# Low parts of input weights: subtracted on GpSimd, or added by a transfer onto a negated copy

## Chip, cores and metric

One NeuronCore of a Trainium2 chip. The metric is device time in microseconds of one execution; the median of three runs is given, and one more execution is profiled.

## What is computed

A trunk of two layers on 512 tokens of 1024 features, in float32. Each layer projects its input `x` by one matrix of 4300 columns into the queries, keys and values of three groups of attention heads (differential, top-128 sparse with an index scorer, forgetting) and a gate. Queries and keys of the first two groups are rotated (rope). The gated outputs go through one output matrix and a layer norm.

```python
def hybrid_layer(x, w_in, ...):
    h = jnp.einsum('bsd,de->bse', x, w_in)
    (dq, dk, dv, sq, sk, sv, iq, ik, iw, fq, fk, fv, ff, gate) = split_columns(h)
...
    mixed = jnp.concatenate([a, bo, co], axis=-1) * jax.nn.silu(gate.astype(jnp.float32))
    out = jnp.einsum('bse,ed->bsd', mixed.astype(x.dtype), w_out)
    return layer_norm(DEEPNORM_ALPHA * x + out, ln_g, ln_b)
```

The time of each layer begins with the einsum on `w_in`, whose weights are what the change touches.

## The kernel before, in words

Every matmul on weights is done in three passes: input and weight are each split into a high part (rounded to `F32R`) and a low part (the rest), and high times high, low times high and high times low are summed in PSUM. So each weight block needs a high tile `whi` and a low tile `wlo`.

`Weights.prep` (line 499) prepares one block of `w_in`, at most 128 x 1024 numbers, 512 KB: SP loads it into `raw` (`dma`, line 364), ScalarE writes `whi` from `raw` (`act`, line 337), and `split` (line 386) has `wlo = raw - whi` computed by whichever of VectorE and GpSimd would end first by the planner's account (`either`, line 377; GpSimd is preferred by a bias, `PREP_BIAS` for most blocks). There are two `raw`, four `whi` and four `wlo` buffers. `prefetch` (line 544) prepares a block three groups ahead of its use. `columns` and `v_group` (lines 553 and 647) issue the matmuls of a group once its parts are ready; the value groups `dv` and `fv` consist of two or three blocks that are needed one right after the other. The output weights have a preparation of their own (`prep_out`, line 514), with `split`.

The work of a layer starts with the groups of `HEAD`: shared keys, `dk`, `dq`, `dv`, then the index queries `iq` 1, 0, 3, 2. `rope` (line 615) turns a projection into query or key tiles: ScalarE copies PSUM to a `tg` tile, SP exchanges its 32-row blocks by four small transfers, products and sums with cosine and sine run on VectorE and GpSimd, and `query_tiles` or `key_tiles` (lines 581 and 591) split the result into `qk` tiles, the low parts on GpSimd or VectorE. `forget` (line 808) runs some twenty tiny operations on `lt` tiles on GpSimd. `index_scores` (line 866) takes the `iq` tiles in order and is the first to need `iq` 0.

All five engines run in an order written down beforehand. `Flow` (line 107) plays the program through: tasks of different priority issue instructions, `issue` (line 221) gives each a start by when its operands and its engine are free, and at the end every engine's instructions are emitted by planned start (`emit`, line 236). On the chip each engine takes its instructions in that order, and each waits for its operands' semaphores; one that waits holds up what is behind it on its engine.

Of the kernel before, what the change touches and what calls it, by code (L numbers as in the profile page):

```python
# [10 lines left out]
AF = mybir.ActivationFunctionType  # L11
OP = mybir.AluOpType
# [37 lines left out]
PREP_BIAS = 3500  # L50
# [56 lines left out]
class Flow:  # L107
# [113 lines left out]
    def issue(self, engine, cost, outs, ins, emit, size=0, port=False):  # L221

        t = max(self.now, self.depends(engine, outs, ins))
        if engine == "pe":
            self.cold = self.cold or t + COLD
            self.now = t + (cost if t >= self.cold else 2 * cost)
        else:
            t = self.slot(engine, t, cost, port)
        end = t + cost
        if engine == "sp":  # L230
            end = self.slot("dma", end + 650, size / 360.0) + size / 360.0
        self.record(engine, end, outs, ins)
        self.order.append((t, len(self.order), emit))
        return end + {"pe": 0, "act": 300, "dve": 260, "pool": 200, "sp": 1040}[engine]

    def emit(self):
        for _, _, f in sorted(self.order, key=lambda o: o[:2]):
# [57 lines left out]
def tile_hybrid_decoder(  # L295
# [17 lines left out]
    nc = tc.nc  # L313
# [8 lines left out]
    flow = Flow()  # L322


    def width(ap):
        n = 1
        for d in ap.shape[1:]:
            n *= d
        return n

    def is_ap(v):
        return isinstance(v, bass.AP)

    def in_psum(ap):
        return ap.tensor.name.split("_")[0] in BANKS

    def act(o, i, func=AF.Copy, **kw):
        acc = [kw["accum_out"]] if "accum_out" in kw else []
        ptr = [v for k, v in kw.items() if is_ap(v) and k != "accum_out"]
        cost = 0.833 * width(o) + (51 if in_psum(i) else 93) + 93 * (len(acc) + len(ptr)) + (125 if o.shape[0] < 128 else 0)  # L340
        return flow.issue("act", cost, [o] + acc, [i] + ptr,
                          lambda: nc.scalar.activation(o, i, func, **kw))  # L342
# [9 lines left out]
    def two_ports(name, o, ins):  # L352

        if name == "scalar_tensor_tensor" and len(ins) == 3:
            ins = [ins[0], ins[2]]
        if name in ("tensor_tensor", "scalar_tensor_tensor"):
            return len(ins) == 2 and not any(in_psum(v) for v in ins)
        return name in ("tensor_scalar", "tensor_copy") and width(o) % 2 == 0 and not any(in_psum(v) for v in ins + [o])
# [5 lines left out]
    def dma(o, i):  # L364
        inside = [v for v in (o, i) if not v.tensor.name.startswith(("in_", "out_"))]
        outs, ins = [v for v in inside if v is o], [v for v in inside if v is i]
        return flow.issue("sp", 640 if ins else 475, outs, ins, lambda: nc.sync.dma_start(o, i),  # L367
                          width(o) * o.shape[0] * 4)

    def mm(o, lhsT, rhs, **kw):  # L370
        flow.issue("pe", width(o) / 2.262 + 2, [o], [lhsT, rhs],
                   lambda: nc.tensor.matmul(o, lhsT, rhs, **kw))  # L372
# [4 lines left out]
    def either(o, a, b, op, bias=BIAS):  # L377

        def end(engine, cost):
            port = engine == "pool" or two_ports("tensor_tensor", o, [a, b])  # L380
            return flow.free_at(engine, max(flow.now, flow.depends(engine, [o], [a, b])), cost, port) + cost
        late = in_psum(a) or in_psum(b) or \
            end("pool", 2.15 * width(o) + 125) > end("dve", 1.04 * width(o) + 69) + bias
        return (vec if late else pool)("tensor_tensor", o, a, b, op=op)

    def split(hi, lo, src, bias=BIAS):
        flow.set("high", act(hi, src))
        return either(lo, src, hi.bitcast(F32), OP.subtract, bias)

    def bank(tag):  # L390
        tag = SHARE.get(tag, tag)
        flow.banks[tag].remove(min(flow.banks[tag]))
        return flow.tile(ps.tile([128, 512], F32, name=tag, tag=tag, bufs=BANKS[tag]), tag, 0, True)

    def tile_of(shape, tag, bufs=0, dt=F32):
        n = bufs or RINGS[tag]
        return flow.tile(sb.tile([128] + shape, dt, name=tag, tag=tag, bufs=n), tag, n, not bufs)
# [45 lines left out]
    def xT_from(l, t, src, ready):  # L443
        for kk in range(2):
            yield "at", ready[kk]
            yield "bank", "t", 1
            pt = bank("t")
            for k in range(4):
                transpose(pt[:, k * 128:(k + 1) * 128], src[kk][:, k * 128:(k + 1) * 128])
            p3 = pt.rearrange("p (k n) -> p k n", k=4)  # L450
            r = split(xh[:, kk * 4:kk * 4 + 4, t * 128:(t + 1) * 128],
                      xl[:, kk * 4:kk * 4 + 4, t * 128:(t + 1) * 128], p3)
            flow.unbank("t", pt)
            yield
        flow.set(("xT", l, t), r)

    def warm():

        z0, z = small([256], "junk", 2)[:, :128], tile_of([256], "junk", 2, F32R)[:, :128]
        vec("memset", z0, 0.0, rate=0.52)  # L460
        yield "at", vec("tensor_copy", z, z0)
        yield "bank", "t", 1
        o = bank("t")[:, :256]
        while "started" not in flow.ev:
            mm(o, z, z[:, :1].to_broadcast([128, 256]), start=True, stop=True)
            yield
        flow.unbank("t", o)

    def load_x():
        yield "take", "pt", NB  # L470
        tiles, at = [], {}
        for k in range(KT):
            if k % 2 == 0:
                tiles.append(tile_of([2, 512], "pt"))
            raw = tiles[-1][:, k % 2]
            dma(raw, xT[k * 128:(k + 1) * 128, :])
            at[k] = split(xh[:, k], xl[:, k], raw, 0)
            flow.set(("x", k), at[k])
            flow.set(("xh", k), flow.ev["high"])
            if k % 2 == 0:  # L480
                prefetch(k // 2)
        for t in range(NB):
            flow.set(("xT", 0, t), max(at.values()))
            flow.give("pt", tiles[t])
        dma(cst[:, :1024], shape_consts[:, :1024])
        yield "at", 10000
        dma(cst[:, 1024:], shape_consts[:, 1024:])
        small_constants()


    class Weights:
# [7 lines left out]
        def prep(self):  # L499
            raw, hi, lo = [tile_of([KT * 128], tag, bufs, dt)[:, :self.n].rearrange("p (k c) -> p k c", k=len(self.ks))  # L500
                           for tag, bufs, dt in (("raw", RAW, F32), ("whi", WHI, F32R), ("wlo", WLO, F32R))]
            src = bass.AP(tensor=w_packed.tensor, offset=self.at, ap=[[self.n, 128], [1, self.n]])
            src = src.rearrange("p (k c) -> p k c", k=len(self.ks))
            self.hi, self.lo, self.ready = {}, {}, {}
            parts = len(self.ks) if self.at == 0 else 1
            for part in range(parts):
                c = slice(part, part + 1) if parts > 1 else slice(0, len(self.ks))
                dma(raw[:, c], src[:, c])
                ready = split(hi[:, c], lo[:, c], raw[:, c], 0 if self.early else PREP_BIAS)
                self.high = flow.ev["high"] if part == 0 else self.high  # L510
                for i, k in list(enumerate(self.ks))[c]:
                    self.hi[k], self.lo[k], self.ready[k] = hi[:, i], lo[:, i], ready
# [40 lines left out]
    def columns(l, w, pp, a, b):  # L553
        for t in range(a // 128, b // 128):
            yield "ev", ("xT", l, t)
        yield "at", max(w.ready.values())
        o = pp[:w.m, a:b]
        for k in range(KT):
            mm(o, w.hi[k], xh[:, k, a:b], start=(k == 0), stop=False)
            mm(o, w.hi[k], xl[:, k, a:b], start=False, stop=False)  # L560
            mm(o, w.lo[k], xh[:, k, a:b], start=False, stop=(k == KT - 1))
            yield
# [786 lines left out]
```

## Time and profile before

| | us |
|---|---|
| runs (3), median | 638.66 (636.81 to 639.17) |
| profiled execution, own time | 640.08 |
| its span | 638.3 |
| TensorE (PE) busy | 604.4 |
| VectorE (DVE) busy | 451.4 |
| ScalarE (ACT) busy | 393.9 |
| GpSimd (POOL) busy | 379.1 |
| granted TensorE clock, mean | 0.978 |

Busy times are those in which an instruction of the engine runs. Matmuls overlap and their ends are modelled, so a busy TensorE is not one at its peak; what counts for it is where it stood idle and for whom. A wait is put down to the instruction whose semaphore came last. The clock is the share of TensorE's full speed that was granted: 1.0 is 2.4 GHz, 0.5 is 1.2 GHz.

### The profile page before, as it was taken

The numbers are of one execution on the slowest core, as the hardware profiler recorded it, in microseconds if no ns is written. First come the engines' busy times: TensorE is split into PE (matmuls) and PEld (weight loads), VectorE is DVE, ScalarE is ACT, GpSimd is POOL, SyncE is SP. The second block draws the span as 40 slices with busy tenths as digits, with TensorE's granted clock in tenths as the row PEclk, the third lists the DMA queues.
The fourth block names the chain that finished last, engine by engine and source line by source line (L and its number), as shares of the span: only waits on it lengthen the run. The fifth ranks groups of instructions, "written<-read, shape, count | busy, mean of one in ns | idle before, by whom it ended". The sixth has DMA issues, their size and how long they took to land.

```text
span 638.3 us, 10384 instructions
## 1 busy us (share of the span) xinstructions
PE 604.4 (95%) x3385; PEld 530.9 (83%) x3385; DVE 451.4 (71%) x1181; ACT 393.9 (62%) x953; POOL 379.1 (59%) x296
## 2 busy tenths in 40 slices
PE   8999599999999799999999797999999999999994
PEld 7899489888988588888899796898888888888884
DVE  4647478999989885774652455799899898556555
ACT  4557486758567579942334676774857768987210
POOL 0178862436848665383646888414676798546824
PEclk9998899999999999999999987999999999999998
DMA  8464223242243321537135442413253253225502
GB/s 315 140 181 124 80 78 101 67 116 76 74 144 105 99 85 66 176 117 229 56 115 134 118 146 63 124 34 99 88 131 109 88 142 107 67 67 182 182 33 100
DMA packets 32198, 72.68 MB, mean 114 GB/s; under 512 B 5392, under 2 KB 6928, under 8 KB 32144
## 3 DMA queue, kind: packets, MB, share of 16 engines
q1 hardware_dynamic: 32144, 72.02, 37.2%
q8 instruction: 27, 0.44, 0.3%
q14 instruction: 27, 0.22, 0.1%
HBM read 53.13 MB, written 4.19 MB: 90 GB/s over the span
## 4 chain that ended last, share of the span: by engine, by line
PE 61%; POOL 8%; DMA 8%; ACT 8%; DVE 6%; issue 5%; SPq 3%; DVEq 0%; POOLq 0%; ACTq 0%
PE w L372 57%; DMA raw<-in_w_packed_dram 4%; PE w L375 4%; POOL tg L362 4%; SPq L367 3%; POOL qk L362 2%; ACT qk L342 2%; ACT p L342 2%; ACT whi L342 2%; DMA tg<-tg 2%; DMA qk<-qk 2%; DVE tg L350 1%; DVE acc L350 1%; POOL wlo L362 1%; POOL p L362 1%
## 5 line engine op out<-in xcount | busy, mean ns | idle before, releaser
L362 POOL TENSOR_TENSOR wlo<-raw,whi 128x1024 fp32r<-128x1024 f32 (+1 forms) x64 | 153.9, 2408 | 103.8 <-ACT whi L342 79.6
L372 PE MATMUL w<-xh,whi 128*128 128x512 f32 (+2 forms) x456 | 178.9, 393 | 2.6 <-ACT p L342 2.5
L372 PE MATMUL w<-xh,wlo 128*128 128x512 f32 (+2 forms) x456 | 171.0, 376 | 1.8 <-POOL wlo L362 1.8
L372 PE MATMUL w<-xl,whi 128*128 128x512 f32 (+2 forms) x456 | 170.9, 376 | 0.0
L372 PEld LDWEIGHTS w<-xh,wlo 128*128 128x128 f32 x456 | 87.0, 191 | 16.6 <-POOL wlo L362 2.1
L372 PEld LDWEIGHTS w<-xh,whi 128*128 128x128 f32 x456 | 87.3, 192 | 14.6 <-ACT p L342 3.3
L342 ACT ACTIVATE whi<-raw 128x1024 fp32r<-128x1024 f32 (+3 forms) x77 | 79.8, 1038 | 29.9 <-DMA raw<-in_w_packed_dram 29.3
L372 PEld LDWEIGHTS w<-xl,whi 128*128 128x128 f32 x456 | 87.5, 192 | 9.8
L372 PE MATMUL w<-qk 128*128 128x256 f32 (+3 forms) x352 | 75.5, 343 | 17.5 <-POOL qk L362 14.1
L362 POOL TENSOR_TENSOR qk<-tg,qk 64x512 fp32r<-64x512 f32 (+1 forms) x59 | 72.5, 1229 | 30.4 <-ACT qk L342 28.0
L372 PEld LDWEIGHTS w<-qk 128*128 128x128 f32 x352 | 59.8, 200 | 25.5 <-POOL qk L362 16.2
L372 PE MATMUL w<-whi,xh 128*128 128x256 f32 (+2 forms) x240 | 75.7, 316 | 0.7 <-ACT p L342 0.7
L372 PE MATMUL w<-wlo,xh 128*128 128x256 f32 (+2 forms) x240 | 75.1, 313 | 0.5 <-POOL wlo L362 0.5
L372 PE MATMUL w<-whi,xl 128*128 128x256 f32 (+2 forms) x240 | 74.9, 312 | 0.0
L342 ACT ACTIVATE p<-w,negm 128x128 f32<-128x128 f32 (+3 forms) x96 | 49.8, 523 | 21.7 <-DVE negm L350 21.3
L350 DVE MAX8 m<-acc 128x8 f32<-128x256 f32 (+2 forms) x96 | 52.6, 552 | 0.1
L350 DVE CUSTOM_DVE_ANT_0 w<-w,cst 128x128 f32<-128x128 f32 (+3 forms) x104 | 47.5, 492 | 7.1 <-PE w L372 6.7
L350 DVE MATCH_REPLACE8 acc<-m,acc 128x512 f32<-128x512 f32 (+2 forms) x96 | 52.1, 543 | 0.0
L342 ACT ACTIVATE qk<-tg 64x512 fp32r<-64x512 f32 (+1 forms) x60 | 35.9, 599 | 25.5 <-POOL tg L362 24.7
L350 DVE TENSOR_TENSOR pt<-w,pt 128x128 fp32r<-128x128 f32 (+3 forms) x96 | 45.0, 484 | 8.1 <-ACT pt L342 7.2
L342 ACT ACTIVATE pt<-w 128x128 fp32r<-128x128 f32 (+3 forms) x96 | 40.0, 438 | 16.6 <-PE w L375 16.2
L362 POOL TENSOR_TENSOR tg<-tg,cst 128x512 f32<-128x512 f32 (+1 forms) x24 | 30.3, 1262 | 33.4 <-DMA tg<-tg 33.2
(132 smaller groups left out, 1152.3 us busy)
## 6 DMA issues: line engine op xcount, KB each, us to landing
raw<-in_w_packed_dram SPq DMA_DIRECT2D x61, 512.0 KB, 3.8
raw<-in_w_out_dram SPq DMA_DIRECT2D x16, 512.0 KB, 3.4
qk<-qk SPq DMA_DIRECT2D x56, 128.0 KB, 2.3
tg<-tg SPq DMA_DIRECT2D x88, 64.0 KB, 2.0
pt<-in_xT_dram SPq DMA_DIRECT2D x8, 256.0 KB, 5.9
raw<-in_w_packed_dram SPq DMA_DIRECT2D x4, 498.0 KB, 4.6
tg<-tg SPq DMA_DIRECT2D x32, 48.0 KB, 2.0
vv<-in_ln_g_dram SPq DMA_DIRECT2D x2, 512.0 KB, 5.9
```

The lines of the kernel that those rows point to most:

```text
L342: lambda: nc.scalar.activation(o, i, func, **kw))
L350: lambda: getattr(nc.vector, name)(o, *args, **kw), port=two_ports(name, o, ins))
L362: lambda: getattr(nc.gpsimd, name)(o, *args, **kw), port=name != "memset")
L367: return flow.issue("sp", 640 if ins else 475, outs, ins, lambda: nc.sync.dma_start(o, i), width(o) * o.shape[0] * 4)
L372: lambda: nc.tensor.matmul(o, lhsT, rhs, **kw))
L375: flow.issue("pe", 109.0, [o], [i, ident], lambda: nc.tensor.transpose(o, i, ident))
```

## The change

For blocks of `w_in` that are not marked early, the low part is no longer computed by a subtraction. ScalarE writes `whi` from `raw`, then writes the same rounding with its sign turned into `wlo`; then GpSimd issues a DMA that reads the block once more from HBM and adds it onto `wlo`, so that it holds the block minus its high part. Early are the first nine blocks of layer 0 and the first three of layer 1; these keep `split`, as do the output weights. That leaves 56 blocks for the new way. In the planner, `issue` now tells an engine that issues a transfer from the queue that moves it, so that a transfer from GpSimd takes time in both; it counts 1100 ns of GpSimd for the issue. `either` no longer has a use of `PREP_BIAS`. The diff, whole but for what surrounds it:

```diff
@@ class Flow, issue
         end = t + cost
-        if engine == "sp":
+        by = "sp" if size else engine
+        if size:
             end = self.slot("dma", end + 650, size / 360.0) + size / 360.0
-        self.record(engine, end, outs, ins)
+        self.record(by, end, outs, ins)
         self.order.append((t, len(self.order), emit))
-        return end + {"pe": 0, "act": 300, "dve": 260, "pool": 200, "sp": 1040}[engine]
+        return end + {"pe": 0, "act": 300, "dve": 260, "pool": 200, "sp": 1040}[by]
...
+    def dma_add(o, i):
+
+        return flow.issue("pool", 1100, [o], [o], lambda: nc.gpsimd.dma_start(o, i, accum_op=OP.add),
+                          6 * width(o) * o.shape[0])
...
+    def split_weights(hi, lo, raw, src):
+
+        flow.set("high", act(hi, raw))
+        act(lo, raw, AF.Copy, scale=-1.0)
+        return dma_add(lo, src)
...
                 dma(raw[:, c], src[:, c])
-                ready = split(hi[:, c], lo[:, c], raw[:, c], 0 if self.early else PREP_BIAS)
+                if self.early:
+                    ready = split(hi[:, c], lo[:, c], raw[:, c], 0)
+                else:
+                    ready = split_weights(hi[:, c], lo[:, c], raw[:, c], src[:, c])
```

Since the planner sees other costs, the order changes on all engines. Three places follow.

GpSimd in layer 0, before the change, from the end of the forget-gate run (`lt`) to the low parts of the second index query `iq` 0 (`qk_223`, `qk_224`); `tg_157` belongs to `iq` 1, `tg_200` to `iq` 0:

```order
L362 TENSOR_TENSOR lt3_145<-lt2_144,lt3_145 128x16
L362 TENSOR_TENSOR wlo_160<-raw_158,whi_159 128x1024
L362 TENSOR_TENSOR tg_157<-tg_157,cst_66 128x384
L362 TENSOR_TENSOR tg_156<-tg_156,tg_157 128x384
L362 TENSOR_TENSOR qk_195<-tg_156,qk_195 64x384
L362 TENSOR_TENSOR qk_196<-tg_156,qk_196 64x384
L362 TENSOR_TENSOR wlo_204<-raw_202,whi_203 128x1024
L362 TENSOR_TENSOR rr_230<-rr_230,ssq_163 128x4
L362 TENSOR_TENSOR wlo_219<-raw_217,whi_218 128x1024
L362 TENSOR_TENSOR tg_200<-tg_200,tg_201 128x384
L362 TENSOR_TENSOR qk_223<-tg_200,qk_223 64x384
L362 TENSOR_TENSOR qk_224<-tg_200,qk_224 64x384
```

And the same place with the change:

```order
L363 TENSOR_TENSOR lt3_145<-lt2_144,lt3_145 128x16
L373 DMA wlo_154<-in_w_packed_dram 128x1024
L363 TENSOR_TENSOR tg_157<-tg_157,cst_66 128x384
L363 TENSOR_TENSOR tg_156<-tg_156,tg_157 128x384
L373 DMA wlo_160<-in_w_packed_dram 128x1024
L363 TENSOR_TENSOR qk_205<-tg_156,qk_205 64x384
L363 TENSOR_TENSOR qk_206<-tg_156,qk_206 64x384
L373 DMA wlo_203<-in_w_packed_dram 128x1024
L363 TENSOR_TENSOR tg_200<-tg_200,cst_66 128x384
L363 TENSOR_TENSOR tg_199<-tg_199,tg_200 128x384
L363 TENSOR_TENSOR qk_224<-tg_199,qk_224 64x384
L363 TENSOR_TENSOR qk_225<-tg_199,qk_225 64x384
```

`wlo_154`, the low part of `iq` 2, was subtracted within the forget-gate run before and is now added behind it; `wlo_219` and the sum `rr` have moved behind `iq` 0, and the product with the sine (`cst`) of `iq` 0 has come from VectorE to GpSimd. `wlo_151`, of `iq` 3, stands within the forget-gate run both times.

ScalarE at the start of layer 1, around the second and third block of `dv` (`raw_881`, `raw_886`), before:

```order
L342 ACTIVATE tg_889<-w_875 128x512
L342 ACTIVATE whi_882<-raw_881 128x996
L342 ACTIVATE whi_887<-raw_886 128x664
L342 ACTIVATE tg_898<-w_876 128x512
L342 ACTIVATE vv_903<-w_905 128x128
```

And with the change:

```order
L343 ACTIVATE tg_889<-w_875 128x512
L343 ACTIVATE whi_882<-raw_881 128x996
L343 ACTIVATE wlo_883<-raw_881 128x996
L343 ACTIVATE whi_887<-raw_886 128x664
L343 ACTIVATE wlo_888<-raw_886 128x664
L343 ACTIVATE tg_898<-w_876 128x512
```

The two copies stand right behind the high parts, ahead of `tg_898`, the start of the third rotation.

GpSimd at the same place, before:

```order
L362 TENSOR_TENSOR wlo_883<-raw_881,whi_882 128x996
L362 TENSOR_TENSOR wlo_888<-raw_886,whi_887 128x664
L362 TENSOR_TENSOR tg_885<-tg_885,cst_66 128x512
L362 TENSOR_TENSOR tg_884<-tg_884,tg_885 128x512
L362 TENSOR_TENSOR qk_892<-tg_884,qk_891 64x512
```

And with the change:

```order
L373 DMA wlo_883<-in_w_packed_dram 128x996
L363 TENSOR_TENSOR tg_885<-tg_885,cst_66 128x512
L373 DMA wlo_888<-in_w_packed_dram 128x664
L363 TENSOR_TENSOR tg_884<-tg_884,tg_885 128x512
L363 TENSOR_TENSOR qk_892<-tg_884,qk_891 64x512
```

The last `dv` block's add now stands between the two first operations of a rotation.

## Rows read from the trace of the kernel before

**Rows 1.** The page's head: span, and busy time of each engine.

```profile
span 638.3 us, 10384 instructions
...
PE 604.4 (95%) x3385; PEld 530.9 (83%) x3385; DVE 451.4 (71%) x1181; ACT 393.9 (62%) x953; POOL 379.1 (59%) x296
```

**Rows 2.** The page's chain that ended last, by engine.

```profile
PE 61%; POOL 8%; DMA 8%; ACT 8%; DVE 6%; issue 5%; SPq 3%; DVEq 0%; POOLq 0%; ACTq 0%
```

**Rows 3.** The waits, TensorE alone: total us, times, longest.

```profile
PE w L372 <- POOL qk L362: 14.1, 8, 7.1
```

**Rows 4.** Stretches: length, busy us (instructions) of each engine, granted clock, DMA share, GB/s.

```profile
40.00:80.00 40.00, 31.12 (x173) 29.57 (x172) 21.25 (x60) 23.67 (x63) 34.43 (x42) 0.88 0.41 121
340.00:400.00 60.00, 52.52 (x291) 49.22 (x290) 29.27 (x84) 38.06 (x94) 52.26 (x55) 0.91 0.40 118
230.00:262.00 32.00, 32.00 (x185) 27.59 (x184) 20.32 (x64) 28.70 (x85) 17.82 (x13) 1.00 0.20 66
540.00:580.00 40.00, 40.00 (x229) 34.56 (x228) 24.56 (x74) 36.96 (x100) 21.07 (x14) 1.00 0.17 53
73.70:80.50 6.80, 3.96 (x12) 3.37 (x13) 2.66 (x5) 3.48 (x9) 5.30 (x6) 0.50 0.00 0
387.70:394.60 6.90, 6.33 (x23) 5.60 (x22) 3.88 (x7) 5.38 (x15) 6.11 (x6) 0.51 0.00 2
```

**Rows 5.** Groups: `whi` by form; `wlo` by tile (ns min/median/max); `wlo` in 40:77.

```profile
L342 ACT ACTIVATE whi<-raw 128x1024 fp32r<-128x1024 f32 x69 | 72.9, 1058 | 22.8 <-DMA raw<-in_w_packed_dram 22.4
...
L362 POOL TENSOR_TENSOR wlo<-raw,whi x64: 1604/2401/2842, 50.3 to 589.4; 128x1024 fp32r<-128x1024 f32 x61, 128x996 fp32r<-128x996 f32 x2, 128x664 fp32r<-128x664 f32 x1
...
L362 POOL TENSOR_TENSOR wlo<-raw,whi 128x1024 fp32r<-128x1024 f32 x5 | 11.9, 2377 | 0.1
```

**Rows 6.** Timeline in layer 0, 54 to 77 us: start, duration, instruction, [idle before].

```profile
54.65 1.05 ACT L342 ACTIVATE whi<-raw 128x1024 fp32r<-128x1024 f32 x1
...
60.80 2.38 POOL L362 TENSOR_TENSOR wlo<-raw,whi 128x1024 fp32r<-128x1024 f32 x1
...
63.81 0.35 PE L372 MATMUL w<-xh,wlo 128*128 128x384 f32 x1
...
76.27 0.79 PE L372 MATMUL w<-qk 128*128 128x256 f32 x2 [7.08 <-POOL qk L362]
```

**Rows 7.** Timeline at the start of layer 1, 341 to 389 us.

```profile
341.16 0.76 ACT L342 ACTIVATE whi<-raw 128x664 fp32r<-128x664 f32 x1 [2.72 <-DMA raw<-in_w_packed_dram]
...
343.66 0.42 PE L372 MATMUL w<-wlo,xh 128*128 128x332 f32 x1 [0.49 <-POOL wlo L362]
...
360.74 0.44 PE L372 MATMUL w<-qk 128*128 128x128 f32 x2 [1.04 <-POOL qk L362]
...
362.08 1.14 PE L372 MATMUL w<-qk 128*128 128x128 f32 x7 [0.90 <-POOL qk L362]
...
365.85 0.45 PE L372 MATMUL w<-xh,wlo 128*128 128x384 f32 x1 [1.76 <-POOL wlo L362]
...
387.35 0.50 PE L372 MATMUL w<-qk 128*128 128x256 f32 x2 [2.71 <-POOL qk L362]
388.42 0.80 PE L372 MATMUL w<-qk 128*128 128x256 f32 x2 [0.57 <-POOL qk L362]
```

**Rows 8.** The page's DMA queues, and DMA issues with median us to landing.

```profile
q1 hardware_dynamic: 32144, 72.02, 37.2%
...
raw<-in_w_packed_dram SPq DMA_DIRECT2D x61, 512.0 KB, 3.8
...
tg<-in_x_dram SPq DMA_DIRECT2D x4, 256.0 KB, 8.3
```

**Rows 9.** Timeline of SP at 63 us: one issue of a weight load.

```profile
63.21 0.33 SPq L367 DMA_DIRECT2D raw<-in_w_packed_dram  x1
```

**Rows 10.** Timeline: high part of a `v` group's last block, its first low-part matmul.

```profile
150.75 1.07 ACT L342 ACTIVATE whi<-raw 128x1024 fp32r<-128x1024 f32 x1
...
161.62 0.28 PE L372 MATMUL w<-wlo,xh 128*128 128x256 f32 x1
```

## Prediction

> **What bounds the kernel now.** I read the page's busy times first, then the waits of TensorE, then stretches of the span, then single instructions at the two places where TensorE stands. TensorE (PE) is busy for 604.4 of 638.3 us, ScalarE (ACT) for 62% and GpSimd (POOL) for 59% [rows 1]. So nothing that merely makes POOL or ACT emptier on average is worth anything; only work that TensorE waits for is. Of the chain that ended last, TensorE holds 61% and POOL 8% [rows 2]. TensorE's largest wait is for POOL's `qk` tiles, 14.1 us in 8 waits, the longest 7.1 [rows 3]: these are the low parts of rotated queries and keys. The stretches show where: in 40 to 80 us POOL is busy for 34.43 of 40 us and TensorE for only 31.12; in 340 to 400 us POOL for 52.26 of 60 and TensorE for 52.52 [rows 4]. These are the two layer starts, where many rotations and weight preparations fall together. Behind the two longest gaps the granted clock is 0.50 or 0.51, its lower level of 1.2 GHz, for 6.8 and 6.9 us [rows 4]; TensorE had stood idle just before. In 230 to 262 and 540 to 580 us TensorE is never idle; there ACT is the fullest engine, 28.70 of 32 and 36.96 of 40 us [rows 4].
>
> **What the change does, part by part.** 56 subtractions `wlo<-raw,whi` leave POOL (a few ran on VectorE in other places and stay there). In their place stand 56 ACT copies `wlo<-raw` and 56 adding transfers that POOL issues. The output weights, the nine first groups of layer 0 and the first three of layer 1 keep the subtraction.
>
> *POOL relieved.* A subtraction holds POOL for some 2.4 us (median 2401 ns [rows 5]); an issue of a DMA is not in the trace of POOL. Bounds: SP's issue of the same load took 0.33 us [rows 9]; at the top the 2.4 us of the subtraction itself. I take 1.2, nearer the lower row, since that one is an issue too and the other is arithmetic on 1024 columns.
>
> *A new latency.* Before, a low part was ready one subtraction after its high part. Now it takes a copy (1.06 us, the high part's 1058 ns [rows 5], half the columns less for the small groups), the issue and the transfer. Call L the time from POOL's issue to the landing. Lower bound: the plain load of 512 KB lands 3.8 us after its issue [rows 8], and an add can't be quicker than the load it contains. Upper bound: 8.3 us, the slowest kind of load in the trace [rows 8]. I take 6: the load's 3.8 plus a second pass over 512 KB for reading the target. All DMA engines were busy for 37.2% of 638.3 us, 237 us, for 72.02 MB [rows 8], so 0.52 MB is 1.7 us; that makes 5.5, and half a microsecond for the issue being on another engine.
>
> By the Trainium skill ("Collectives: The Full Stack", section "The bandwidth ceiling: the fold count and why AG ≠ RS ≠ AR") an adding transfer is slowed by its two source reads and not by the addition, to about half a copy's rate; with that alone L would be 5.5 and the forecast half a microsecond lower. No row of this trace can show it.
>
> *Layer 0, 40 to 77 us.* Five subtractions of 2.38 us, 11.9 us in all, stand on POOL here [rows 5], all ahead of the `qk` tile for which TensorE stands 7.08 us until 76.27 [rows 6]. In the new order four issues (4 x 1.2 = 4.8) and a rope product that VectorE did (about 1.0) are ahead of it. Relief: 11.9 - 5.8 = 6.1 us, so the gap falls to about 1.0. Is the low part in time that TensorE needs just before, that of `iq` 2? Its high part ends at 55.70 [rows 6], the copy at 56.8, but its add stands behind the whole forget-gate run on POOL. That run ended at 60.80 [rows 6] with two subtractions in it; with one issue in their place it ends at 60.80 - 4.8 + 1.2 = 57.2, and the add lands at 63.2, wanted at 63.81 [rows 6]. It just fits at L = 6, and up to 1 us more hides in the gap that is left. Besides, the slow clock from 73.70 covers 3.96 us of busy TensorE, of which half is loss [rows 4]; the gap that is left may still bring some of it, so I count 1.0 of 2.0. Gain: 7.1 us.
>
> *Layer 1, 337 to 395 us.* Here the change costs first. The three groups of `dv` are adding ones. The last one's high part ends at 341.92, and its low part was wanted at 343.17, when TensorE stood for it until 343.66 [rows 7]. Now: 341.92 + 0.76 for the copy + 6 = 348.7, that is 5.0 us later; as it is a smaller block I take 4.6. Behind it lie the gaps of 1.04, 0.90 (two `qk` waits) and 1.76 us (an `iq` low part) [rows 7]. The first two close, because the key rotations now lead TensorE and POOL has shed two subtractions ahead of them; the third, again a low part with little margin, turns into a wait of about 1.0 more. So -4.6 + 3.7 - 1.0 = -1.9. Then POOL sheds five more subtractions before the index scores: 5 x (2.4 - 1.2) = 6.0 us against a gap of 2.71 and one of 0.57 [rows 7]: +3.3. The slow clock behind it covers 6.33 us of busy TensorE [rows 4], 3.2 lost, and I count 2.4 of it, with what the gaps near 365 cost. Layer 1: +3.8.
>
> *ACT.* 56 copies of 1.06 us are 59 us more on an engine that idles for 38% of the span [rows 1]; they hide, except where ACT is full. Two copies fall in each of the two full stretches, 4.2 us; between 0 (TensorE has projections to fill with) and 4.2. I take 2.0, the middle.
>
> *SP and DMA.* SP keeps every transfer. A raw buffer comes free after the copy and no longer after the subtraction, so loads start earlier. The adds take DMA time where the mean load is 37.2% [rows 8]; rope exchanges may be delayed by part of an add. No separate term. Elsewhere the margin is wider: in a tight `v` group TensorE reached the low part at 161.62, 9.8 us after the high part's end at 151.82 [rows 10], and copy plus add, 7.1 us, hide.
>
> *Sum.* 7.1 + 3.8 - 2.0 = 8.9 us, against the profiled execution's 640.1 us: 631.2. It stood 1.4 us above the runs' median of 638.7, so I say 631.
>
> **The rivals.**
> *Late adds (slower).* Each us of L beyond 6 is paid at the layer starts, and beyond about 9 the `v` groups wait too, with their 9.8 us from high part to first use [rows 10]. Place: the first low part after each layer start. At L = 9 the layer-0 gap is refilled (7.1 - 3) and layer 1 loses 3 more on the first `dv` wait and some on the `iq` ones: the sum is near 0. At L = 12: layer 0 keeps about 1, layer 1 is at -7, ACT -2, four `v` groups wait 1.5 each: -14, 654 us. For it: a transfer that reads, adds and writes back has no row here, and the first `dv` group has under 2 us to spare. Against it: loads of 512 KB land at 3.8. It decides from L of about 9.
>
> *No relief on POOL (same to slower).* If an issue holds POOL for 2.4 us, the gaps at 76 and 387 stay and the `dv` wait comes on top: layer 0 +0.5, layer 1 -1.9 - 1.2, ACT -2: 644.7. One mechanism would be that POOL can write descriptors only while VectorE is not working: VectorE is busy for 21.25 of the 40 us [rows 4], which would stretch 1.2 to 1.2 / 0.47 = 2.6. Against it: POOL's own subtractions were hardly held up, median 2401, longest 2842 ns [rows 5].
>
> The Trainium skill ("SBUF — State Buffer", section "🔬 SBUF: two separate sides", the box "The 'DVE blocks DMA' trap (SWDGE)") warns of just this: a DMA issued by GpSimd is starved of descriptors while VectorE runs an operation that takes both ports. It names single-source copies, which are few here.
>
> *Half of it (a small gain).* The gap at 76 may close only to where iq 0's own rope chain ends, or only one layer start gains: 636.
>
> **How the numbers follow.** No change that is under 0.5%, 3.2 us, can be told from none here. Forecast 0.56, late adds 0.17, no relief 0.15, half 0.12. Faster by over 0.5% (below 635.5): 0.52 of the forecast and 0.03 of the half case, 0.55. Slower (above 641.9): 0.15 of the late adds and 0.09 of the no-relief case, 0.24. The rest, 0.21, is the same. Range: at the lower bounds (issue 0.33, L 3.8) both gaps close and their clock losses go, layer 0 about 10 and layer 1 about 9.5: 621. At the top, L of 8.3 with a dear issue gives 647 to 648. Beyond it lie most of the late adds, 0.15, and little below: 621 to 648. The forecast's own range is 621 to 636.
>
> **What would show it.** Right: TensorE's wait for `qk` from POOL falls from 14.1 to under 6 us; POOL's share falls by some 10 points; landings of `wlo<-in_w_packed_dram` at a median of 5 to 7 us; a wait of TensorE of 3 to 5 us on the first `dv` low parts of layer 1, released by a DMA. Wrong: a median landing above 9 us or waits on that DMA beyond 10 us in total; POOL rows of over 2 us for an issue; new TensorE waits on ACT in the two full stretches.

## The result, and the profile of the changed kernel

The changed kernel takes 679.22 us (median of 4 runs, 677.17 to 680.98) against 638.58 (4 runs, 636.81 to 639.17): a ratio of 1.0638, 95% interval 1.0608 to 1.0667. It is 40.6 us slower, where 631 was forecast and 621 to 648 given as the range. The profiled execution took 680.42 us, its span 678.6. Of the ten runs of the version with four adds in experiment 8, one, 638.40 us, was in a slower state of the chip and is left out of its ratio.

The page's head, then its chain that ended last, by engine (before: [rows 1, 2]):

```profile
span 678.6 us, 10461 instructions
...
PE 621.2 (92%) x3385; PEld 540.7 (80%) x3385; DVE 443.5 (65%) x1177; ACT 443.7 (65%) x1010; POOL 302.2 (45%) x301
...
PE 44%; ACT 20%; DMA 13%; DVE 8%; issue 5%; POOL 5%; SPq 3%; DVEq 0%; POOLq 0%; ACTq 0%
```

POOL went from 59% to 45% of a longer span, as meant. TensorE stands still for 678.6 - 621.2 = 57.4 us, before for 33.9. Its busy time rose by 16.8 us although it does the same 3385 matmuls: the mean granted clock fell from 0.978 to 0.960, and at half clock (58.20 to 65 us below) one of 128x384 is listed with 0.52 us, after it with 0.34.

TensorE's waits (total us, times, longest), then the second of them in the kernel before, in a fence of its own:

```profile
PE w L378 <- DMA wlo<-in_w_packed_dram: 17.0, 6, 4.1
PE w L378 <- DMA qk<-qk: 14.1, 8, 3.3
PE w L378 <- POOL qk L363: 4.6, 4, 2.3
```

```profile
PE w L372 <- DMA qk<-qk: 3.4, 3, 2.0
```

The wait for POOL's `qk`, 14.1 us before [rows 3], is down to 4.6. Two waits on transfers have taken its place: 17.0 us on the adds, and 14.1 us on the exchanges `qk<-qk`, which the change does not touch (3.4 us before).

DMA queues (packets, MB, share of the time of the 16 engines), and issues with their median us to landing; the second fence is of the kernel before (the rest: [rows 8]):

```profile
q1 hardware_dynamic: 32144, 72.02, 35.3%
q0 software_dynamic: 8064, 29.15, 24.7%
...
raw<-in_w_packed_dram SPq DMA_DIRECT2D x61, 512.0 KB, 4.8
wlo<-in_w_packed_dram POOLq DMA_DIRECT2D x53, 512.0 KB, 6.8
...
qk<-qk SPq DMA_DIRECT2D x56, 128.0 KB, 4.0
tg<-tg SPq DMA_DIRECT2D x88, 64.0 KB, 2.1
...
tg<-tg SPq DMA_DIRECT2D x32, 48.0 KB, 4.4
```

```profile
qk<-qk SPq DMA_DIRECT2D x56, 128.0 KB, 2.3
...
tg<-tg SPq DMA_DIRECT2D x32, 48.0 KB, 2.0
```

The adds (queue q0) hold all 16 engines for 24.7% of 678.6 us, 167.6 us: 3.0 us each, against 1.7 for a plain load of the same size. An add lands 6.8 us after its issue (5.2 to 9.0). The transfers that were there already land later: raw loads 4.8 us (3.8 before), `qk<-qk` 4.0 (2.3), the 48 KB `tg<-tg` 4.4 (2.0). The 88 of 64 KB hardly move in the median, 2.1 (2.0).

Stretches (columns as in [rows 4]). The changed kernel is later at most places, so a stretch is set against the one that holds the same matmuls by their count from the start: 348 to 421 us against 340 to 400 before, 578 to 618 against 540 to 580. The last line is a half-clock stretch in layer 0:

```profile
40.00:80.00 40.00, 34.23 (x184) 30.78 (x182) 19.97 (x58) 27.91 (x68) 27.57 (x43) 0.91 0.70 174
348.00:421.00 73.00, 56.87 (x292) 52.44 (x291) 28.76 (x80) 42.67 (x99) 37.27 (x51) 0.86 0.67 155
578.00:618.00 40.00, 40.00 (x228) 34.39 (x227) 21.41 (x68) 38.02 (x100) 18.69 (x16) 1.00 0.59 150
...
58.20:65.00 6.80, 5.61 (x22) 5.32 (x22) 3.62 (x8) 1.87 (x4) 3.28 (x4) 0.50 1.05 246
```

In layer 0 the change helps: TensorE begins 184 matmuls in these 40 us, 173 before, and is some 2.5 us ahead at their end. At the start of layer 1 POOL fell from 52.26 to 37.27 busy us, and yet the same work takes 73 us in place of 60. Where TensorE never stood before, 540 to 580 us, it does not stand now, though the DMA share there is 0.59 instead of 0.17.

By the same count (good to a microsecond or so, as the order differs) the changed kernel is 8 us behind where the kernel before stands at 340 us, 21 at 400, 38 at 540 and 40.3 at the end. So 13 us are lost at the start of layer 1, where TensorE waits 13.7 us for low parts, and 17 between 400 and 540 us, where it waits for no low part but 6.8 us for `qk<-qk`.

The groups of the add's issue and of the copy:

```profile
L373 POOL DMA_DIRECT2D wlo<-in_w_packed_dram x56 | 49.8, 890 | 164.6 <-ACT wlo L343 94.7
...
L343 ACT ACTIVATE wlo<-raw 128x1024 fp32r<-128x1024 f32 (+2 forms) x56 | 58.5, 1045 | 0.0
```

TensorE's timeline at the places the prediction spoke of, and one in mid layer (start, duration, instruction, idle before):

```profile
59.39 0.69 PE L378 MATMUL w<-xh,wlo 128*128 128x384 f32 x1 [3.24 <-DMA wlo<-in_w_packed_dram]
...
75.11 0.51 PE L378 MATMUL w<-qk 128*128 128x256 f32 x2 [0.83 <-POOL qk L363]
76.19 1.03 PE L378 MATMUL w<-qk 128*128 128x256 f32 x5 [0.57 <-POOL qk L363]
...
219.48 1.73 PE L378 MATMUL w<-qk 128*128 128x128 f32 x6 [3.27 <-DMA qk<-qk]
...
354.05 0.42 PE L378 MATMUL w<-wlo,xh 128*128 128x332 f32 x1 [4.11 <-DMA wlo<-in_w_packed_dram]
357.33 0.65 PE L378 MATMUL w<-wlo,xh 128*128 128x332 f32 x1 [1.34 <-DMA wlo<-in_w_packed_dram]
...
386.99 0.69 PE L378 MATMUL w<-xh,wlo 128*128 128x384 f32 x1 [3.73 <-DMA wlo<-in_w_packed_dram]
```

The 7.08 us gap at 76 [rows 6] is 0.83 + 0.57 now: POOL's relief is real. But TensorE stands 3.24 us at 56.16 for the low part of `iq 3`, and the half-clock stretch from 58.20 follows. At the start of layer 1 five low parts are waited for. The row at 219.48 is of another kind: no add is waited for, a key exchange is. The DMA view of 205 to 220 us tells why; its issues:

```profile
wlo<-in_w_packed_dram POOLq DMA_DIRECT2D x2, 512.0 KB, 7.8
raw<-in_w_packed_dram SPq DMA_DIRECT2D x2, 512.0 KB, 6.1
qk<-qk SPq DMA_DIRECT2D x4, 128.0 KB, 6.2
tg<-tg SPq DMA_DIRECT2D x4, 64.0 KB, 7.0
```

Two adds and two loads are in flight with eight exchanges, and their medians are all 6 to 8 us.

### The profile page after: what moved, and what is told of

Read it like the earlier page. It is cut to its first block, busy times and chain, and to the rows that moved or that the text cites. A ratio compares the mean times of both kernels' runs of the same rounds, so it can differ in the third digit from the quotient of the medians.

```text
span 678.6 us, 10461 instructions
## 1 busy us (share of the span) xinstructions
PE 621.2 (92%) x3385; PEld 540.7 (80%) x3385; DVE 443.5 (65%) x1177; ACT 443.7 (65%) x1010; POOL 302.2 (45%) x301
## 3 DMA queue, kind: packets, MB, share of 16 engines
q0 software_dynamic: 8064, 29.15, 24.7%
## 4 chain that ended last, share of the span: by engine, by line
PE 44%; ACT 20%; DMA 13%; DVE 8%; issue 5%; POOL 5%; SPq 3%; DVEq 0%; POOLq 0%; ACTq 0%
PE w L378 42%; ACT p L343 6%; DMA tg<-tg 4%; SPq L368 3%; DMA wlo<-in_w_packed_dram 3%; ACT whi L343 3%; DMA qk<-qk 3%; DMA raw<-in_w_packed_dram 3%; ACT wlo L343 2%; PE w L381 2%; ACT pt L343 2%; DVE acc L351 2%; POOL qk L363 1%; ACT tg L343 1%; DVE m L351 1%
## 5 line engine op out<-in xcount | busy, mean ns | idle before, releaser
L378 PE MATMUL w<-xh,wlo 128*128 128x512 f32 (+2 forms) x456 | 172.8, 380 | 11.5 <-DMA wlo<-in_w_packed_dram 11.5
L373 POOL DMA_DIRECT2D wlo<-in_w_packed_dram x56 | 49.8, 890 | 164.6 <-ACT wlo L343 94.7
L378 PE MATMUL w<-qk 128*128 128x256 f32 (+3 forms) x352 | 80.4, 352 | 22.3 <-DMA qk<-qk 14.1
L343 ACT ACTIVATE whi<-raw 128x1024 fp32r<-128x1024 f32 (+3 forms) x77 | 79.8, 1037 | 24.2 <-DMA raw<-in_w_packed_dram 23.9
L363 POOL TENSOR_TENSOR qk<-tg,qk 64x512 fp32r<-64x512 f32 (+1 forms) x60 | 75.5, 1258 | 23.8 <-ACT qk L343 20.8
L378 PE MATMUL w<-wlo,xh 128*128 128x256 f32 (+2 forms) x240 | 77.1, 321 | 5.5 <-DMA wlo<-in_w_packed_dram 5.4
L378 PE MATMUL w<-whi,xh 128*128 128x256 f32 (+2 forms) x240 | 77.4, 322 | 1.5 <-DVE tg L351 1.0
L378 PE MATMUL w<-whi,xl 128*128 128x256 f32 (+2 forms) x240 | 76.9, 321 | 1.1 <-DVE xl L351 1.1
L363 POOL TENSOR_TENSOR tg<-tg,cst 128x512 f32<-128x512 f32 (+1 forms) x27 | 33.8, 1250 | 76.5 <-DMA tg<-tg 62.4
L343 ACT ACTIVATE wlo<-raw 128x1024 fp32r<-128x1024 f32 (+2 forms) x56 | 58.5, 1045 | 0.0
L378 PEld LDWEIGHTS w<-wlo,xh 128*128 128x128 f32 x240 | 47.0, 196 | 8.2 <-DMA wlo<-in_w_packed_dram 6.4
```

What stands on the lines that cost most here:

```text
L363: lambda: getattr(nc.gpsimd, name)(o, *args, **kw), port=name != "memset")
L373: return flow.issue("pool", 1100, [o], [o], lambda: nc.gpsimd.dma_start(o, i, accum_op=OP.add), 6 * width(o) * o.shape[0])
```

## The experiments

The theories at the start: *late landing* (TensorE waits for low parts), *traffic* (the adds also slow the exchanges on the same DMA engines), and *copies and order* (ACT's copies, the planner's new order). Single times below are of one profiled run each, against a kernel before of 637 to 641 us on the same chip; the last two versions have ten runs each. The kernel before ran from 635.36 to 639.69 us in 19 runs on one chip, so a difference of under some 4 us between two single runs says nothing. Of the edits the calls that matter are shown, shortened.

**1. Take the traffic away, leave everything else.**

```diff
-nc.gpsimd.dma_start(o, i, accum_op=OP.add)
+nc.gpsimd.dma_start(o[:, :1, :64], i[:, :1, :64], accum_op=OP.add)
```

> The changed kernel with every adding transfer cut to 64 of its columns (128 x 64 instead of 128 x 1024): the rest of each low part keeps the negated high part alone, so most of the low part's sum is left out. Order on all engines, copies on ACT, issues on POOL and the waits stay; the traffic of the adds goes, and the landing comes sooner (about 2 to 3 us after the issue). Theory 'late landing' (TensorE waits for low parts at the layer starts and nothing else matters): the 17.0 us of TensorE's waits on wlo go, and with them some 10 us of half clock: 650 to 656. Theory 'traffic' (the adds also hold up the small exchanges qk<-qk and tg<-tg on the shared DMA engines): besides the above, TensorE's wait on DMA qk<-qk falls from 14.1 to 5 or less: 630 to 643. Theory 'copies and order' (ACT's 56 copies and the planner's new order cost the time): stays above 662.

Measured: 638.57 us. Waits of TensorE and two landings:

```profile
PE w L378 <- POOL qk L363: 6.6, 6, 3.1
PE w L378 <- DMA qk<-qk: 2.8, 2, 1.4
...
PE w L378 <- DMA wlo<-in_w_packed_dram: 1.4, 2, 1.0
...
qk<-qk SPq DMA_DIRECT2D x56, 128.0 KB, 2.3
...
tg<-tg SPq DMA_DIRECT2D x32, 48.0 KB, 1.9
```

Copies, issues and order are those of the changed kernel, and it is as quick as the kernel before. *Copies and order* is out as what cost the time. All of the 40.6 us hangs on moving the data, by its traffic or by its landing (3.2 us after the issue here), and the exchanges are back at their old times.

**2. Put the traffic back, onto DRAM, with nobody waiting; and a control for the second issue.**

```diff
-nc.gpsimd.dma_start(o, i, accum_op=OP.add)
+nc.gpsimd.dma_start(o[:, :1, :64], i[:, :1, :64], accum_op=OP.add)
+nc.gpsimd.dma_start(aside(o), i, accum_op=OP.add)
```

`aside(o)` is an array in DRAM that nothing reads.

> Like the kernel with the adds cut to 64 columns, and behind each of these POOL issues the whole add once more onto an array in DRAM that nothing waits for: the traffic is back (though to DRAM), the wait for it is not; most of each low part is again left out, and POOL has 56 issues more (some 50 us of its idle time). Theory 'late landing': near the kernel with the cut adds, within 6 us. Theory 'traffic': 12 to 25 us above it, with raw loads near 4.8 us, qk<-qk near 4.0 us from issue to landing and TensorE's wait on DMA qk<-qk back at 10 us or more. Theory 'copies and order': both the same, above 662.

> Control for the kernel that issued a small add and then a whole one onto DRAM: both adds have 64 columns here, so POOL has the same 112 issues and hardly any traffic; most of each low part is left out. Theory 'traffic': 638 to 645, so that at least 35 of the 44 us between that kernel and the one with the cut adds are the traffic. Rival 'the second issue on POOL costs it': above 660.

Measured: 682.58 us, and 658.52 for the control, whose second add has 64 columns too. Both expectations were missed: the first is 44 us above the cut adds and not 12 to 25, and the control, awaited at 638 to 645, is just under the 660 of its rival: 56 more issues on POOL, 1.21 us each, cost 20 us with hardly any traffic (the exchanges `qk<-qk` land in 2.4 us there). Between the two the traffic makes 24 us; how much it makes with fewer issues this pair doesn't say.

**3. Tell the planner the landing; keep the subtraction where adds were late.** The first adds 3000 ns to the planned landing of an add, the second raises the count of blocks that keep the subtraction.

> The changed kernel with the planner told that an add lands 3.0 us later than it had assumed (about 8 us from issue to landing in place of 5), so that TensorE's work is ordered for it; the computation is the same. Theory 'late landing': most of the 17.0 us of waits on wlo is filled with other work: 655 to 665. Theory 'traffic': the wlo waits fall, the waits on qk<-qk and the slower exchanges stay: 662 to 674. Theory 'copies and order': the order is what costs, so it may move by 10 us either way.

> The changed kernel with the subtraction kept also for one more group of layer 0 (iq 3) and for the first 12 blocks of layer 1, those whose adds landed late; 42 or so adds stay. Theory 'late landing': the waits on wlo go, those of TensorE on POOL's qk come back in part (before: 14.1 us): 648 to 656. Theory 'traffic': the second half of each layer still suffers (TensorE's waits on DMA qk<-qk near 10 us), but the layer start of layer 1 has its exchanges back: 655 to 668. Theory 'copies and order': within 8 us of the changed kernel's 679.

Measured: 674.55 and 657.14 us. In the first, TensorE's wait on `wlo` falls from 17.0 to 5.4 us, but the time by 4.7 only, little more than the scatter; 9.5 us of waits on `qk<-qk` stay. In the second no wait on `wlo` is left, 46 adds are, and TensorE waits 11.0 us on `qk<-qk`. *Traffic* put them at 662 to 674 and 655 to 668: the first is half a microsecond above, the second within. The second lies only 1 us above the range of *late landing*, too, and it drops adds as well as waits: ten adds fewer, nine of them at the start of layer 1, are worth 22 of the 40.6 us.

**4. What of the traffic: bytes, the adding, the time on the engines, or the size of its pieces?** Half the columns; a plain load (no `accum_op`); rows of 1 KB (`max_dma_last_dim=1024`).

> The changed kernel with each add cut to half its columns (128 x 512; the other half of each low part keeps the negated high part alone). Theory 'traffic, in proportion to the time on the DMA engines': half way between the adds of 64 columns (638.6 us) and the whole ones (679.2): 655 to 662; landing near 5 us, tg<-tg and qk<-qk near 3 us. Rival 'only a long transfer hurts, since exchanges must wait behind it': below 648, with the exchanges at 2.3 us or less.

> The changed kernel with a plain load of the same 512 KB from POOL in place of each add (it overwrites the negated high part with the whole weight, so the low part is left out). Same issues, same bytes written, but no second read. Theory 'time on the DMA engines': a plain load took 1.7 us of all 16 engines per 512 KB and an add 3.0 (97 us in place of 168 in all), so 638.6 + 40.6 x 0.55 = 661, and 652 to 666 as a range; landing 4 to 5 us. Rival 'the bytes count': within 5 us of 679. Rival 'it is the adding itself that holds others up': below 646.

> The changed kernel with each add made of rows of 256 columns (1 KB) in place of 1024 (4 KB): the same sums and bytes in four times as many pieces. Theory A 'an exchange waits behind one piece of the add at a time': the pieces are a quarter, the exchanges tg<-tg and qk<-qk come back to 2.5 to 3 us, the time falls to 650 to 668, unless POOL's issue becomes much dearer (0.9 us now; it could be up to 3.6). Theory B 'the engines are shared by time': exchanges stay at 4 us or more, 676 to 690.

Measured: 650.70, 649.37 and 678.98 us. The queue of the adds in the half, the plain and the finely cut kernel, in this order:

```profile
q0 software_dynamic: 8064, 14.75, 14.0%
```

```profile
q0 software_dynamic: 8064, 29.15, 14.5%
```

```profile
q0 software_dynamic: 29568, 29.15, 28.6%
```

Half an add and a plain load hold the engines for about the same time (14.0% of 648.9 us and 14.5% of 647.6, 91 and 94 us) and cost the same, though the one moves half the bytes and the other adds nothing. That speaks for the time on the engines, and against the bytes and the adding. It is no clean test: both land sooner than a whole add (5.0 and 4.5 us, for 6.8), and a plain load's issue holds POOL for 0.59 us in place of 0.89. Nor is the cost in proportion; both times lie below their ranges. Against the kernel before, 22 us on the engines (64 columns) cost nothing, some 92 cost 11, and 168 cost 40. Cutting the adds into pieces of 1 KB gains nothing: `qk<-qk` stays at 4.1 us, as theory B said; but these adds also hold the engines longer, for 28.6% of 677.2 us, 194 us. The Trainium skill ("DMA: Bandwidth & Descriptors", section "🔬 Queues, rings and completion order") states that an engine takes turns between queues by whole packets of several descriptors, not by single ones. The run with small pieces speaks against turns by single pieces, but no run here shows how many pieces a packet holds.

**5. Take the exchanges `tg<-tg` away, in both kernels.**

```diff
-    t = dma(hs[32 * b:32 * b + 32, :], g[32 * (b ^ 1):32 * (b ^ 1) + 32, :])
+    t = dma(hs[32 * b:32 * b + 32, :], g[32 * (b ^ 1):32 * (b ^ 1) + 32, :], False)
...
-    either(hs, hs, sinT[:, c], OP.mult)
+    either(hs, hs, sinT[:, c], OP.mult, read=g)
```

With `False` the transfer is planned but not issued; with `read=g` the product reads `g` in its place.

> The changed kernel without the 120 transfers tg<-tg: the product with the sines reads the tile itself and not the exchanged halves, so every rotation is left half undone; order and everything else stay. With the control below (the same in the kernel before). Theory 'the adds hurt through the late exchanges': the fall from 679 is larger than the control's by 8 us or more: 645 to 668. Rival 'through the late low parts and loads alone': the fall is the control's, 2 to 7 us: 672 to 677.

> Control: the kernel before without the 120 transfers tg<-tg (the rotations left half undone in the same way). Rope chains are 2 us shorter everywhere; TensorE waited 14.1 us for POOL's qk, which these chains feed only in part: 632 to 637 by either theory. If it falls by as much as the changed kernel does, the adds do not act through these exchanges.

Measured: 665.21 us (14.0 less than 679.22) and 636.38 (2.2 less than 638.58). Without these exchanges the change costs 28.8 us in place of 40.6: they carry about 12, give or take 4, as *through the late exchanges* had it (8 or more).

**6. No landing waited for, with and without `tg<-tg`.** The whole add goes onto DRAM, with no small one before it.

> The changed kernel with every whole add sent to an array in DRAM that nothing waits for: 56 issues and about the same time on the DMA engines, but TensorE waits for no landing (the low parts keep the negated high part alone; POOL's issues no longer wait for ACT's copy). Theory 'two parts': the kernels with 112 issues differed by 24 us (682.6 to 658.5) for the traffic alone, so 638.6 + 24 = 663 here, 657 to 668, and the 16 us to 679 are the late landings. Rival 'late exchanges only': 673 or more. Rival 'late landings only': 645 or less.

> The same, and without the 120 transfers tg<-tg besides (the rotations left half undone): neither landings nor these exchanges are waited for; the exchanges qk<-qk and the loads still share the engines with the adds. Theory 'two parts': the tg exchanges were worth 11 to 12 us of the traffic in the changed kernel (14.0 less 1.7 to 2.7 in the control), so 663 - 14 = 649, 644 to 655; what is left above 638 is the key exchanges'. If the traffic hurts in another way than through exchanges and landings (ports, HBM, late loads), it stays at 658 or more.

Measured: 680.09 and 659.45 us. TensorE's first wait in each, and the start of layer 1 in the first:

```profile
PE w L382 <- DMA qk<-qk: 18.1, 9, 4.3
```

```profile
PE w L384 <- DMA qk<-qk: 19.7, 10, 3.7
```

```profile
354.00:414.00 60.00, 52.54 (x289) 48.58 (x288) 26.27 (x80) 42.22 (x97) 34.51 (x50) 0.91 0.76 178
```

"Two parts" fell as a sum: with no low part waited for, the time is the same, in the range of "late exchanges only". But the stretch tells more than the sum. The matmuls at the start of layer 1 take the 60 us of the kernel before, not 73, with eight adds in it and nine before: the 13 us lost there go with waiting for low parts. This run loses as much more elsewhere, 14 us up to this stretch (8 in the changed kernel) and 24 in the next, up to 577 us (17). Why is not shown: its adds fall at other times, since they don't wait for ACT's copy, they write to DRAM, and an issue takes POOL 1.02 us. Taking `tg<-tg` away besides gains 20.6 us. What is left, 659.45, is in the range that was named for another way than exchanges and landings; 19.7 us of waits for key exchanges stand there, so that such a way is neither needed nor excluded.

**7. Key exchanges off the DMA engines.** VectorE copies `qk<-qk` (0.42 us each in the median) in place of the transfers. The planner still counts a transfer, so it leaves no room on VectorE for the copy.

```diff
+def swap(o, i):
+    return flow.issue("sp", 640, [o], [i], lambda: nc.vector.tensor_copy(o.bitcast(F32R), i), width(o) * o.shape[0] * 4)
...
-dma(k[r2:r2 + 64].bitcast(F32), k[r:r + 64].bitcast(F32))
+swap(k[r2:r2 + 64].bitcast(F32), k[r:r + 64].bitcast(F32))
```

> The changed kernel with the 56 key exchanges qk<-qk made as copies by VectorE (64 x 512 across partitions) in place of transfers; the result is the same, the adds and all their traffic stay. Theory 'the adds hurt through the exchanges': TensorE's 14.1 us of waits on DMA qk<-qk go, with some of the half clock behind them: 655 to 668, unless the copies cost VectorE as much (see the control). Rival 'late low parts': 674 or more, with the 17 us of waits on wlo unchanged.

> The same, and without the 120 transfers tg<-tg (rotations left half undone): no exchange uses the DMA engines any more, the adds do. Theory 'through the exchanges': 638 to 652, where what stays above 636 is the wait on late low parts (17 us, which then is the largest of TensorE). Rival 'a third way': 656 or more.

> Control: adds cut to 64 columns (most of each low part is left out) and the key exchanges as copies by VectorE: what the copies cost where the DMA engines are free. 634 to 644 if the copies are hidden, so that the kernel with whole adds and copies can be read as it is; above 648 if they hold VectorE up.

Measured: 677.88, 676.72 and 666.87 us. TensorE's first wait in the first:

```profile
PE w L381 <- DMA wlo<-in_w_packed_dram: 14.1, 6, 4.8
```

The control says that the first two can't be read as they are: the copies cost 28 us where the DMA engines are free. VectorE is busy there for 482.4 us (445.3 in experiment 1) and holds 29% of the chain (8%). The numbers themselves speak against *through the exchanges*: 677.88 is in the range of the rival "late low parts" (674 or more), 676.72 in that of "a third way" (656 or more), and taking `tg<-tg` away gains 1.2 us here, less than the scatter, where it gained 14.0 and 20.6 before. For it speaks only that whole adds cost 677.88 - 666.87 = 11.0 us more than cut ones, against 40.6 with transfers; where VectorE is on the path so often, a part of the harm may be covered. So this experiment decides nothing.

**8. A version that beats both.** Adds for three or four blocks of layer 0 only, and 2000 ns more in the plan for an add's landing.

```diff
+ADDS = [(0, 9), (0, 10), (0, 11), (0, 12)]
...
-                if self.early:
-                    ready = split(hi[:, c], lo[:, c], raw[:, c], 0)
+                if not self.adds:
+                    ready = split(hi[:, c], lo[:, c], raw[:, c], 0 if self.early else PREP_BIAS)
```

> A version to beat both: adds only for three blocks of layer 0 (iq 2, fq 1, fk 1), whose low parts had 5 to 12 us to spare, the subtraction everywhere else; the planner is told that an add lands 2 us later. Three adds are 9 us of DMA time in place of 168. Theory 'the change's own gain at the start of layer 0 is real, and the traffic eats it': TensorE's 7.1 us wait for POOL's qk falls to 2 or less, time 629 to 636. Rival 'POOL is only one of several things late there': 636 to 642.

> The same with iq 3 added, whose add landed 3.2 us late in the changed kernel. By the first theory 628 to 636, if its landing (6 to 7 us with little traffic) is hidden by the new order; 634 to 642 if it is waited for.

Measured over 10 runs each, against 637.47 us (19 runs): three adds 634.80 us, ratio 0.9958 (0.9937 to 0.9980); four 634.28, ratio 0.9937 (0.9905 to 0.9969); by the ratios 2.7 and 4.0 us less. Both lie in the ranges of the first theory, though the longest wait for POOL's `qk` fell from 7.1 us to 3.7 and 3.5 and not to 2. In the profile with four, TensorE's first wait and the start of layer 0:

```profile
PE w L379 <- POOL qk L364: 9.0, 7, 3.5
```

```profile
40.00:80.00 40.00, 34.13 (x191) 30.68 (x190) 22.41 (x65) 29.13 (x72) 29.90 (x43) 0.96 0.67 173
```

With four, TensorE is busy for 34.13 us there, before 31.12 [rows 4], at a clock of 0.96 instead of 0.88. In the profile with three it is not (30.92 us): its wait for POOL's `qk` there fell from 8.9 to 4.2 us, but one of 4.4 us for a high part came in. The idea pays a little where POOL is what is waited for: 3 to 4 us, where 7.1 were forecast for this place.

## Why the prediction was wrong, point by point

- **"SP and DMA ... No separate term": this step failed.** The text itself took a second pass over 512 KB, another 1.7 us, for an add, so some 3.4 us on the engines (it measured 3.0), and said that rope exchanges "may be delayed by part of an add"; then it put the mean load of 37.2% in place of a price. 56 x 3.0 = 168 us more on engines that were busy for 237, in the same stretches as loads and exchanges, cost the whole of the 40.6 us (experiment 1, where hardly any data moves). Two ways are seen. TensorE waits for late low parts, above all at the start of layer 1, where adds land after some 8 us: 13 us are lost there, and none in the run in which nothing waits for a landing (experiment 6). And exchanges come late: `qk<-qk` landed 1.7 us later in the median, in 205 to 220 us 3.9 later, and TensorE waits for them for 9.5 to 19.7 us in each run with 46 or more whole adds that kept them as transfers; without `tg<-tg` the change costs 12 us less (experiment 5). How the other 27 us split among exchanges and anything else stays open, as the parts do not add up (experiments 6 and 7). Late weight loads are not it by the waits: ACT stands 23.9 us for `raw`, before 29.3.
- **POOL relieved: right.** An issue took 0.89 us (1.2 was taken, the sum of 56 is 49.8 us), and the wait on `qk` fell from 14.1 to 4.6 us, under the 6 that were named.
- **L: right in size in the median, 6.8 us for 6**, within the bounds 3.8 to 8.3; but the 512 KB adds at the start of layer 1 took 7.9 to 8.6. The terms there were worked out with one L for every place.
- **Layer 0, +7.1.** The gap closed as worked out, but the text looked at `iq 2` alone. The add of `iq 3` started at 51.84, landed 7.5 us later, and TensorE waited 3.24 us; the clock of 0.50 behind it ran over 5.61 us of busy TensorE, by the text's own reckoning half lost. Some 2.5 us of gain were left at 80 us, and 3 to 4 us in a kernel with few adds.
- **Layer 1, +3.8: its start took 13 us longer.** The sum has a slip of its own: it counts the third gap, 1.76 us, among the closed ones, and also as growing by 1.0. The price on the first `dv` low parts, 4.6, was near (4.11 and 1.34 in two waits). The wait of about 1.0 on a later `iq` low part became three, 2.41, 3.73 and 2.15 us, which ate the gain on the gaps and put the clock down behind them.
- **ACT, -2.0.** It can't be read alone. But with the traffic gone the whole sum was 0 and not +8.9 (638.57 us, experiment 1): POOL's `qk` still held TensorE for 6.6 us, and small waits for VectorE and ACT came in. ACT's share of the chain was 14% there, 8% before. So the gains were too large as well, or ACT's price too small; which is not shown.
- **The rivals.** *Late adds* had the sign, and the time that it gave, 654 at L = 12, was still 25 us short, at an L that was never reached. At 8 us, where layer 1 begins, its reasons held in part. Adds that delay other transfers were not on the list. *No relief on POOL* is refuted by the 0.89 us of an issue.
- **What would show it wrong** did: waits on the adds' DMA came to 17.0 us, over the 10 that were named.

## What to carry to other kernels

Work that is moved from an engine to the DMA queues is not free because the mean DMA share is low: multiply the number of transfers by their time on all 16 engines and look, stretch by stretch, at which small transfers on a dependency chain share it. Here the harm grew faster than the added load (experiment 4), and an adding transfer held the engines 1.8 times as long as a plain one (168 us against 94 for 56 of each). Use it for the few places where the relieved engine is what is waited for, and where its landing is covered. And set stretches of two kernels side by side by the work in them, not by their times: the stretch from 540 to 580 us holds other work once the kernel is 38 us late.

## What was not expected of the hardware

- Cutting an add's rows from 4 KB to 1 KB left the exchanges as late as before (4.1 us); POOL's issue became dearer, 1.32 us in place of 0.89, and the adds held the engines for 194 us in place of 168. A plain 512 KB load took POOL 0.59 us, an add onto DRAM 1.02, or 1.21 right behind another add.
- 56 extra issues of 1.21 us on a POOL that is busy for half of the span cost 20 us, 0.36 us each. POOL's share of the chain rose from 8% (experiment 1) to 13%: its idle time was not all spare.
- 22 us of extra transfers cost nothing against the kernel before, 92 cost 11, 168 cost 40. The `qk<-qk` exchanges landed in 2.3, 2.6 to 2.8 and 4.0 us.
